# A fourth pair of output tiles by seven quarter products, with two pairs summed in PSUM

## The chip, the cores and the metric

The kernel runs on one core of a Trainium2 chip. TensorE multiplies, VectorE and ScalarE work on elements, GpSimd (POOL) and SyncE (SP) mostly start transfers. The metric is the device time of one execution in microseconds (us); the time of a kernel is the median of its runs.

## The reference

One decoder layer over 1024 tokens of width 1024, in float32:

```
h = rmsnorm(x) * (1 + scale(c)) + shift(c)
cv, cg, cs, lx, ls = split(h @ w_in)              # five blocks of 1024 columns
v = conv31(cv * sigmoid(cg))                      # causal, depthwise
v = silu(layernorm(v));  y_conv = (v @ pw2 + b) * silu(cs)
xs = conv4(lx);  r, i = sigmoid(xs @ wr), sigmoid(xs @ wi)     # eight heads
hs = scan(exp(-8 r softplus(-lam)), ...);  y_lru = hs * silu(ls)
x = x + (1 + gate(c)) * (concat(y_conv, y_lru) @ w_out)
out = rmsnorm(x, final_g)
```

The change is in the lru half of the last product, `y_lru @ w_out[1024:]`: eight output tiles of 128 channels by 1024 tokens, each a sum over eight blocks k of 128 rows of `w_out`.

## The kernel before

Channels lie on the partitions, tokens on the free axis; a half is 512 tokens, and one PSUM bank holds one half of a tile. Every float32 operand is split into a high part (`whi`, `yh`) and a remainder (`wlo`, `yl`), and a product is three matmuls: high by high (H), high by remainder (X), remainder by high (W). The order of all instructions on all engines comes from a planner written into the kernel (`Plan`): every operation has a priority (its slot number, with offsets), a cost, and the buffers that it reads and writes; the planner lays the operations out in time and emits them in that order. A PSUM tile `mm` has two banks (three such tiles), a tile `acc` has one (two of them); SBUF tiles come from a pool of 47 `big` buffers of 128x1024 and from smaller pools for weights (`raw`, `whi`, `wlo`, two of each). The planner keeps a reader and a writer of one PSUM tile apart in time (`o.psum`, `clear`); the semaphores that the instructions really wait for are put in afterwards by the tile framework, which looks at tiles.

The stages in order of slots: input products and gates (slots 0 to 39), the lru half of the output product (slots 40 to 47), the product with `pw2` (48 to 55), the conv half of the output product (56 and on), the last normalisation. The layer norm over the convolved channels (`conv_sum`, `layer_norm`, tiles `mean`, `lnss`, `lnbc`) and the operands for `pw2` (`quarters`) are made on VectorE and ScalarE during slots 40 to 47.

Output tiles 0 to 5 are made in pairs (`lru_pair`, `LRU_P = 3`). In a pair, blocks k = 0 to 3 (`JS = (0, 1)`) go by a scheme of seven quarter products in place of eight: with rows in two groups, columns in two halves, and the weight combinations S1 to S4 (`lsh`, `lsl`, made early by `lru_prepare` and kept in HBM) and operand combinations T1 to T4 (`yhs`, `yls`, made by `lru_sums`), the products are 1 = A11 B11, z = A12 B21, y = S1 T1, 2 = S2 T2, 3 = S3 T3, s = S4 B22, 4 = A22 T4. Each is two blocks by three matmuls of 512 columns. Product x goes on accumulating 1, 2, 3, 4 in one bank, and after each step `use` adds the running sum into one of the four quarters of the SBUF tiles `acc`, on ScalarE (the first time, `LACT`) or VectorE. Blocks k = 4 to 7 (`rest`) are multiplied directly (letters p, q, r). The order of a pair is `LORDER = "p1zy2q3s4r"`. It uses three PSUM tiles: `lp` (both halves of the first output tile), `lx` (of its two banks only the first) and `ly` (an `acc` tile). Tiles 6 and 7 (slots 46, 47) are made directly, as `ps`: 8 blocks by 3 matmuls by 2 halves, 48 matmuls each. A finished `acc` tile is added to `accd` in HBM by a transfer from POOL (`acc_store`).

A remainder is made either by VectorE (`SUB`) or by ScalarE and a transfer that adds (`remainder`): ScalarE writes minus the high part, POOL starts a transfer that adds the full value from HBM.

Of the kernel before, what the change touches and what calls it, by code (L numbers as in the profile page):

```python
# [14 lines left out]
P = 128  # L15
D = 1024
T = 1024
# [59 lines left out]
NP = {0: (6, 0, 1), 512: (6, 0, 7), 768: (6, 0)}  # L77
SUMS = (2, 0, 4, 3, 1, 6, 7, 5)
CSD = 2
SPILL = (0,2,4)  # L80
# [12 lines left out]
PREN, PRES = 5, 3  # L93
PREP, XCP = 18, 19
# [1 line left out]
XCN = 33  # L96
LEV = ()
LWB = "big"
LWO = 0.5
FINP = -0.5  # L100
BCLATE = False
BEHIND = 0
PLACED = ("big",)
MARGINS = 2.0
TERMS = {**{("pw2_0", c): ("HW", "X") for c in "1z"}, **{(f"out_{p}", "1"): ("HX", "W") for p in (0, 1, 2, 3)}, **{(f"pw2_{p}", "1"): ("HX", "W") for p in (1, 2, 3)}}
LTERMS = {}
LLATE = 45
SLOTT = {46: ("HX", "W"), 47: ("HX", "W")}
FINQ = 0.0
LRV = ()  # L110
QRES = 0
SINGLE = (0,)
AHEAD = 4
# [45 lines left out]
class Plan:  # L159
# [23 lines left out]
    def op(self, eng, cost, emit, prio, r=(), w=(), table=None, after=(), reserve=0,  # L183
           columns=0, lock=False, lag=0.0, moved=0.0, flight=FLIGHT):
        o = Op()
        o.lag, o.moved, o.flight = lag, moved, flight
        o.eng, o.cost, o.emit, o.prio, o.table = eng, cost, emit, prio, table
        o.succ, o.ready, o.seq, o.reserve = [], 0.0, len(self.ops), reserve
        o.columns = columns
        o.lock = not lag and eng == "POOL" or eng == "DVE" and lock  # L190
        r, w = list(self.keys(r)), list(self.keys(w))
        preds = set(after)
        for k in r:
            if k in self.writer:
# [166 lines left out]
def hymba_layer(ctx: ExitStack, tc: tile.TileContext, xT, vecs, mod_w, w_first, w_in,  # L361
# [214 lines left out]
    def mm_tile(name, parts=2):  # L576
        return S.buf("mm", name, F32, parts)
# [192 lines left out]
    def rstd(prio, sqs, a, e, ps, o, after=(), warm=(), idle=None):  # L770


        nb = (e - a) // P
        sd, rs = S.buf("sd", f"sd{prio}_{o}"), S.buf("rs", f"rs{prio}_{o}")
        wk = halves(ps, o, o + e - a)


        def warm_mm():
            pe.matmul(half(idle, 0)()[:, :P], ones, ones, start=True, stop=True)

        def stats(sq, k):
            for b in range(nb):
                pe.matmul(ps()[:, o + b:o + b + 1], sq()[:, a + b * P:a + b * P + P],
                          ones[:, 0:1], start=k == 0 and b == 0, stop=k == len(sqs) - 1,
                          skip_group_check=True)

        def spread(ps=ps):
            for b in range(nb):
                pe.matmul(ps()[:, o + b * P:o + b * P + P],
                          rs()[:, b:b + 1].to_broadcast([P, P]), ident, start=True, stop=True)  # L790
# [7 lines left out]
        inverse[a] = S.op("DVE", 0.2, lambda: dve.reciprocal(rs()[:, :nb], sd()[:, :nb]), prio, [sd], [rs])  # L798
# [478 lines left out]
    def gates(i, n):  # L1277
# [27 lines left out]
        o = split(B0 - 2 + 0.2 * i, yh[i], yl[i], t, reserve=SPARE)  # L1305
        if i < YHEADS:
            waiting.append(o)
        if LRU_P and i // 2 in JS:
# [2 lines left out]
                lru_sums(i // 2)  # L1311

    def lru_sums(j):
        pr, x0, x1 = B0 - 2 + 0.4 * j + LTP, ys[2 * j], ys[2 * j + 1]

        def sub(to, a, b):
            TT(pr, "DVE", half(*to), half(*a), half(*b), ALU.subtract, H, r=[a, b], w=[to])
        sub((x0, 0), (x0, 1), (x0, 0))
        sub((x0, 1), (x1, 1), (x0, 1))
        sub((x1, 1), (x1, 1), (x0, 0))  # L1320
        sub((x1, 0), (x1, 0), (x1, 1))
        sets = []
        for z, x in enumerate((x0, x1)):
            hi, lo = (big_buf(f"y{h}s{j}{z}", F32R, 2) for h in "hl")
            if j in LTD:
# [57 lines left out]
    def lru_pair(p, n, use, firsts):  # L1383
        rest = LK[2 * NJ:]
        s0, s1 = ("lru", 2 * p), ("lru", 2 * p + 1)
        q = n - 1.4 - LWO
        for s in (s0, s1):
            w_bufs(s, LWB)
            DMA(n - 2.5 - LWO, k3(raw[s]), lambda s=s: wsrc(s)[:, :, :], FULL_BYTES, w=[raw[s]])
        r0, r1 = raw[s0], raw[s1]  # L1390
        for s, k in ((s0, 0), (s1, NJ)):
            hi, lo, r = whi[s], wlo[s], raw[s]
            cut = lambda b, k=k: (lambda: k3(b)()[:, k:, :])
            keys = lambda b, k=k: [(b, i) for i in range(k, KT)]
            ACT(q, cut(hi), cut(r), "copy", (KT - k) * P, r=keys(r), w=keys(hi))
# [8 lines left out]
        for h, t in zip("hl", (sh, sl)):  # L1404
# [1 line left out]
        wq = {"S3": (sh, sl, 0, 0), "S4": (sh, sl, 1, 0), "S2": (sh, sl, 2, 0), "S1": (sh, sl, 3, 0),  # L1406
              "A11": (whi[s0], wlo[s0], 0, None), "A12": (whi[s0], wlo[s0], 1, None),
              "A22": (whi[s1], wlo[s1], 1, None)}
        p0, x, y = mm_tile(f"lp{p}"), mm_tile(f"lx{p}"), acc_tile(f"ly{p}")
        g, ops = 0.0, {}  # L1410

        def quarter(c, a, b, ps, h, begin):
            wh, wl, i, key = wq[a]
            rk = [(wh, key), (wl, key)] if key is not None else kk(wh, i) + kk(wl, i)
            for j, (bh, bl) in enumerate(lsets[b]):
                def emit(j=j, bh=bh, bl=bl):
                    o = (i * NJ + j) * P
                    for lhs, rhs, t in ((wh, bh, 0), (wh, bl, 1), (wl, bh, 2)):
                        pe.matmul(half(ps, h)(), lhs()[:, o:o + P], half(*rhs)(),  # L1419
                                  start=begin and j == 0 and t == 0, stop=j == NJ - 1 and t == 2,  # L1420
                                  skip_group_check=True)
                o = S.op("PE", 3 * (H + 32) / 2400, emit, n + g, [*rk, bh, bl],
                         [(ps, h if ps.parts > 1 else 0)], columns=3 * H)
                ops.setdefault(c, o)

        for c in LORDER:
            g += 0.12
            if c == "p":
                groups = LTERMS.get(p, ("HXW",))
# [90 lines left out]
    for s in slots[4:]:  # L1520
# [5 lines left out]
        if s[0] == "pair":  # L1526
# [14 lines left out]
            started[n], started[n + 1] = lru_pair(s[1], n, use, [started[n - 2]])  # L1541
            for m, t in zip((2 * s[1], 2 * s[1] + 1), ts):
                acc_store(n, m, t)
            n += 1
            continue
        if s not in NEXT:
            if s[0] == "lru":
                weights(s, n=n - LWO, eng="DVE" if s[1] in LRV else "DMA", where=LWB,
                        later=[started[LLATE]] if LLATE else [])
            else:  # L1550
                weights(s, late=[pending_evac[n]] if n in pending_evac else ())
# [243 lines left out]
```

## Time and profile before

| | |
|---|---|
| median of 3 runs | 726.79 us (726.64 to 727.24) |
| profiled execution | 726.9 us, of which the span of its instructions is 725.1 us |
| mean granted TensorE clock | 0.995 |
| TensorE matmuls | busy 717.0 us, 99% of the span |
| VectorE | 617.8 us, 85% |
| ScalarE | 480.8 us, 66% |
| lru half of the output product | from 470 to 558 us of the span |
| product with `pw2` | from 558 to 631 us |
| after the last conv products of 512 columns | from 704 us on |

Busy time of matmuls overlaps from one to the next: a matmul of 512 columns shows 389 ns, and the next one starts about 227 ns after it. How evenly TensorE is fed is read from the starts.

### The profile page before, as it was taken

To read this page: it belongs to the slowest core of one execution; us is meant where nothing else is said; L and a number is where in the kernel's file an instruction comes from. 1 tells how busy PE (TensorE), PEld (TensorE's weight loads), DVE (VectorE), ACT (ScalarE), POOL (GpSimd) and SP (SyncE) were. 2 spreads that over 40 slices of the span, in tenths; PEclk is the share of its full clock that TensorE was granted. 3 is DMA by queue.
4 is the path that set the end of the run, shared out by engine and by line. 5 is a ranking of instruction groups with operands and counts; after the bars stand their busy time and mean duration, and the time that the engine had idled before them with its cause. 6 is when DMAs were issued, how large, how long until landed. Compare 5 with 4: busy or idle time off the path is not lost.

```text
span 725.1 us, 9076 instructions
## 1 busy us (share of the span) xinstructions
PE 717.0 (99%) x3274; PEld 597.5 (82%) x3274; DVE 617.8 (85%) x848; ACT 480.8 (66%) x615; POOL 170.8 (24%) x172
## 2 busy tenths in 40 slices
PE   9999999999999999999999999999999999999996
PEld 8888888888888888888888888888888888888885
DVE  7999999899799997688499995999789566999656
ACT  7650679655698857966949879858785345755322
POOL 0036233443543320233220220211021101100003
PEclk9999999999999999999999999999999999999997
DMA  9946348768899997799999597998867855774006
GB/s 341 408 169 169 43 112 234 191 120 200 180 246 209 264 220 194 172 221 217 193 217 301 111 188 172 253 239 230 190 103 160 228 120 143 223 190 176 23 17 215
DMA packets 46059, 137.80 MB, mean 190 GB/s; under 512 B 5200, under 2 KB 15824, under 8 KB 45904
## 3 DMA queue, kind: packets, MB, share of 16 engines
q0 software_dynamic: 20016, 54.84, 42.0%
q1 hardware_dynamic: 24992, 81.48, 32.3%
q10 hardware_dynamic: 1008, 0.92, 0.4%
q8 instruction: 25, 0.41, 0.2%
q14 instruction: 18, 0.15, 0.1%
HBM read 79.37 MB, written 21.50 MB: 139 GB/s over the span
## 4 chain that ended last, share of the span: by engine, by line
PE 96%; DVE 1%; ACT 1%; DMA 1%; issue 0%; POOL 0%; POOLq 0%
PE ps L560 57%; PE xout L736 6%; PE xpw L736 6%; PE first L867 5%; PE ypw L736 3%; PE gate L1287 3%; PE lp L560 2%; PE lx L1419 2%; PE zout L736 2%; PE zpw L736 2%; PE ly L560 1%; PE lx L560 1%; PE lp L1419 1%; PE yout L736 1%; PE late L867 1%; PE ly L1419 1%
## 5 line engine op out<-in xcount | busy, mean ns | idle before, releaser
L560 PE MATMUL ps<-uh,whi 128*128 128x512 f32 x576 | 177.4, 389 | 0.0
L560 PE MATMUL ps<-ul,whi 128*128 128x512 f32 x576 | 177.4, 389 | 0.0
L560 PE MATMUL ps<-uh,wlo 128*128 128x512 f32 x576 | 177.3, 389 | 0.0
L560 PEld LDWEIGHTS ps<-uh,wlo 128*128 128x128 f32 x576 | 108.1, 188 | 22.5
L560 PEld LDWEIGHTS ps<-ul,whi 128*128 128x128 f32 x576 | 108.1, 188 | 22.4
L560 PEld LDWEIGHTS ps<-uh,whi 128*128 128x128 f32 x576 | 108.0, 188 | 22.3
L405 ACT CAST whi<-raw 128x1024 fp32r<-128x1024 f32 (+1 forms) x44 | 45.1, 1031 | 48.7 <-PE ps L560 30.0
L437 POOL DMA_DIRECT2D es<-cq x45 | 41.0, 910 | 128.7 <-ACT cq L413 90.2
L432 POOL TENSOR_TENSOR wlo<-raw,whi 128x1024 fp32r<-128x1024 f32 x16 | 41.6, 2607 | 88.6 <-ACT whi L405 88.3
L413 ACT ACT_TABLE_LOAD x45 | 57.7, 1283 | 2.0 <-PEq L1787 0.7
L424 DVE SCALAR_TENSOR_TENSOR cacc<-v,V,cacc 128x511 f32<-128x511 f32 (+14 forms) x75 | 55.8, 744 | 0.5
L424 DVE SCALAR_TENSOR_TENSOR caccs<-v,V,caccs 128x511 f32<-128x511 f32 (+6 forms) x70 | 52.1, 745 | 2.2 <-ACT caccs L413 1.1
L424 DVE SCALAR_TENSOR_TENSOR caccs<-c,wsum,caccs 128x511 f32<-128x511 f32 (+6 forms) x70 | 52.1, 745 | 0.8
L437 POOL DMA_DIRECT2D oo<-co x39 | 37.0, 980 | 41.3 <-issue 10.6
L413 ACT ACTIVATE cq<-v,V 128x511 f32<-128x511 f32 (+14 forms) x45 | 31.8, 709 | 0.0
L424 DVE SCALAR_TENSOR_TENSOR xs<-ps,V,xs 128x1023 f32<-128x1023 f32 (+2 forms) x24 | 30.7, 1278 | 0.0
L424 DVE SCALAR_TENSOR_TENSOR modw<-modw,sc 128x1024 f32<-128x1024 f32 x23 | 29.6, 1289 | 0.2 <-DMA modw<-in_mod_w_dram 0.2
L413 ACT ACTIVATE cq<-c,wsum 128x512 f32<-128x512 f32 x42 | 29.7, 713 | 0.0
L432 DVE TENSOR_TENSOR wlo<-raw,whi 128x1024 fp32r<-128x1024 f32 x20 | 24.4, 1220 | 5.4 <-ACT whi L405 5.2
L413 ACT ACTIVATE co<-v,V 128x510 f32<-128x510 f32 (+12 forms) x39 | 27.0, 707 | 0.0
L413 ACT ACTIVATE finsq<-fin 128x512 f32<-128x512 f32 (+2 forms) x14 | 7.9, 570 | 27.4 <-DVE fin L424 14.3
L432 POOL TENSOR_TENSOR o<-fin,bc 128x256 f32<-128x256 f32 (+1 forms) x8 | 7.8, 994 | 68.6 <-ACT bc L405 63.0
(413 smaller groups left out, 1585.5 us busy)
## 6 DMA issues: line engine op xcount, KB each, us to landing
raw<-in_w_in_dram SPq DMA_DIRECT2D x36, 512.0 KB, 5.5
modw<-in_mod_w_dram SPq DMA_DIRECT2D x24, 512.0 KB, 9.2
scsd<-scs SPq DMA_DIRECT2D x8, 512.0 KB, 3.7
raw<-in_w_out_dram SPq DMA_DIRECT2D x8, 512.0 KB, 7.7
accd<-acc POOLq DMA_DIRECT2D x8, 512.0 KB, 6.9
rawpw<-in_pw_dram SPq DMA_DIRECT2D x8, 512.0 KB, 4.3
scsr<-scsd SPq DMA_DIRECT2D x8, 512.0 KB, 4.5
rawout<-in_w_out_dram SPq DMA_DIRECT2D x8, 512.0 KB, 3.5
```

The lines of the kernel that those rows point to most:

```text
L405: act.copy(out(), in_())
L413: act.activation(out=out(), in_=in_(), func=func, **kw)
L424: dve.scalar_tensor_tensor(out=out(), in0=in0(), scalar=scalar, in1=in1(), op0=op0, op1=op1, accum_out=accum)
L432: lambda: e.tensor_tensor(out=out(), in0=a(), in1=b(), op=op), prio, r, w,
L437: return S.op("POOL", ISSUE, lambda: pool.dma_start(out(), a(), accum_op=ALU.add), prio, r, w, lag=RATE * n / T, after=after, flight=flight)
L560: pe.matmul(ps()[:, a - off:b - off], k3(lhs)()[:, at, :], rhs[k]()[:, a:b], start=(k == first and lhs is wh and rhs is xh and (a - off) % ...
L736: pe.matmul(half(ps, 0)(), half(*lhs)()[:, j * P:j * P + P], half(*rhs)(), start=start and at == 0 and i == 0, stop=at == len(order) - 1 a ...
L867: pe.matmul(ps()[:, a - off:b - off], fw_part(lhs, k, i * P, i * P + P)(), rhs()[:, a:b], start=k == 0 and lhs is wh and rhs is xh, stop=k ...
L1287: pe.matmul(ps()[:, c0:c1], lhs()[:, j, :], rhs()[:, c0:c1], start=st == 0, stop=st == 2)
L1419: pe.matmul(half(ps, h)(), lhs()[:, o:o + P], half(*rhs)(), start=begin and j == 0 and t == 0, stop=j == NJ - 1 and t == 2, skip_group_che ...
```

## The change

Four things are done. (1) Tiles 6 and 7 become a fourth pair (`LRU_P = 4`). (2) Pairs 2 and 3 (`FORKP`) no longer use `ly` and no longer add quarters up in SBUF: quarter product 1 is made in bank 0 of `lx` and copied by ScalarE into bank 0 of `lp`; y is made in bank 1 of `lx` and copied into an SBUF tile `lk`; 2 goes on in bank 0 of `lx`; VectorE adds `lx` bank 0 and `lk` into bank 1 of `lp`, and, after 3, into bank 1 of `lx`; z, s, 4 and the direct products then accumulate on these copies, and each finished output tile of 128x1024 is read out by one ScalarE instruction. For these two tiles the planner counts each bank for itself (`Bank`). (3) Some remainders move to VectorE: those of weights 3, 4, 5 (`LRV`) and of the lru operand combinations of j = 1 (`LTDMA` empty, `LTD` unused). (4) Numbers of the order: `TLATE` from 2.5 to 3.0, `LTP`, `LTJ`, `LWO`; weights of tiles 0 to 4 from the small pools (`LWBS`); groups of H and X before W in pairs 1 to 3 (`LTERMS`) and in some quarters of pair 0 (`QT`); the first four of the eight small matmuls that spread a norm over a tile now set the start flag once for each bank, so that a copy can be accumulated on afterwards.

```diff
-TLATE = 2.5
+TLATE = 3.0
-LRU_P = 3
+LRU_P = 4
-LTP = 0.5
+LORDERS = {}
+LTP = 0.0
+LTJ = (0.0, 0.4)
+LTDMA = ()
-LWO = 0.5
+LWO = 0.7
+FORKP = (2, 3)
+FORKN = -1.0
+FEVAC = ("ACT", "ACT")
+LWBS = (5, 6, 7)
-LRV = ()
+LRV = (3, 4, 5)
...
+        self.banks = None
+class Bank:
+    def __init__(self):
+        self.read, self.written = {}, {}
-        o.psum = [(b, any(k[0] is b for k in w)) for b in o.bufs if b.pool in ("mm", "acc")]
+        o.psum = [(b, any(k[0] is b for k in w)) for b in o.bufs if b.pool in ("mm", "acc") and not b.banks]
+        o.psum += [(k[0].banks[k[1]], k in w) for k in dict.fromkeys(r + w) if isinstance(k[0], Buf) and k[0].banks]
...
-        p0, x, y = mm_tile(f"lp{p}"), mm_tile(f"lx{p}"), acc_tile(f"ly{p}")
+        p0, x = mm_tile(f"lp{p}"), mm_tile(f"lx{p}")
+        y = None if p in FORKP else acc_tile(f"ly{p}")
...
+        if p in FORKP:
+            x.banks, p0.banks = [Bank(), Bank()], [Bank(), Bank()]
+            def both(h, to):
+                TT(n + FORKN, "DVE", half(to, 1), half(x, 0), half(kept, 0), ALU.add, H, r=[(x, 0), kept],
+                   w=[(to, 1)])
...
+            quarter("1", "A11", "B11", x, 0, True)
+            ACT(n + FORKN, half(p0, 0), half(x, 0), "copy", H, r=[(x, 0)], w=[(p0, 0)])
+            quarter("y", "S1", "T1", x, 1, True)
+            kept = big_buf(f"lk{p}")
+            ACT(n + FORKN, half(kept, 0), half(x, 1), "copy", H, r=[(x, 1)], w=[kept])
+            quarter("2", "S2", "T2", x, 0, False)
+            both(0, p0)
+            quarter("z", "A12", "B21", p0, 0, False)
+            plain(s0, p0, 0)
+            quarter("3", "S3", "T3", x, 0, False)
+            both(0, x)
+            quarter("s", "S4", "B22", p0, 1, False)
+            plain(s0, p0, 1)
+            out_of(0, p0)
+            quarter("4", "A22", "T4", x, 0, False)
+            plain(s1, x, 0)
+            plain(s1, x, 1)
+            out_of(1, x)
+            return ops["1"], ops["3"]
```

On TensorE nothing moves ahead of the first lru product, and from the second pair of `pw2` on the rows are the same. Pair 2 before, on TensorE, from its quarter product 1 (`lx`, the operands `yh_3782` and `yh_2187`) to its quarter product s (`lp` with the weights `lsh`); the bracket names the engine whose semaphore a row waits for:

```order
L1419 MATMUL lx_4235<-yh_3782,whi_4104 128x512 [waits Activation_49]
L1419 MATMUL lx_4235<-yh_2187,whi_4104 128x512
L1419 MATMUL lp_4199<-yh_3785,whi_4104 128x512
L1419 MATMUL ly_4145<-yhs_3806,lsh_4082 128x512
L1419 MATMUL lx_4235<-yhs_3866,lsh_4082 128x512 [waits Activation_49]
L1419 MATMUL lx_4235<-yhs_3819,lsh_4082 128x512
L1419 MATMUL lp_4199<-yh_3785,lsh_4082 128x512 [waits DVE_49]
```

(These are the first rows of seven groups of three; the rows between are the X and W matmuls of the same block.) Between the last row of product 1 and the row that waits for ScalarE stand nine matmuls of other tiles, and each of the two waits is for a tile that TensorE left some rows earlier. Pair 2 now, on TensorE, from the end of the first block of y (`lx` with `yhs_3814` and `lsh`, `lsl`) through its second block (`yhs_3047`) to the first block of 2 (`yhs_3849`):

```order
L1448 MATMUL lx_4179<-yhs_3814,lsl_4104 128x512 [waits DMAHW2_49]
L1448 MATMUL lx_4179<-yhs_3047,lsh_4100 128x512 [waits Activation_49]
L1448 MATMUL lx_4179<-yls_3062,lsh_4100 128x512
L1448 MATMUL lx_4179<-yhs_3047,lsl_4104 128x512
L1448 MATMUL lx_4179<-yhs_3849,lsh_4100 128x512
L1448 MATMUL lx_4179<-yls_3861,lsh_4100 128x512
L1448 MATMUL lx_4179<-yhs_3849,lsl_4104 128x512
L1448 MATMUL lx_4179<-yhs_3882,lsh_4100 128x512 [waits Activation_49]
```

and then, from the end of 2 (`yhs_3882`) through the first block of z (`lp` with `yh_3789`) to its second (`yh_3794`):

```order
L1448 MATMUL lx_4179<-yhs_3882,lsl_4104 128x512
L1448 MATMUL lp_4193<-yh_3789,whi_4088 128x512
L1448 MATMUL lp_4193<-yl_3806,whi_4088 128x512
L1448 MATMUL lp_4193<-yh_3789,wlo_4098 128x512
L1448 MATMUL lp_4193<-yh_3794,whi_4088 128x512 [waits DVE_49]
```

Product 1 of `lx` is now followed by y in the other bank of the same tile; the waits stand in the middle of y, of 2 and of z, between two blocks of one product, and no matmul of another tile is between. What is waited for, on ScalarE, in the same place (`lp_4193<-lx_4179` copies product 1, `lk_4205<-lx_4179` copies y):

```order
L433 ACTIVATE acc_4133<-lx_4059,gate_95 128x512 [waits PE_49]
L425 COPY lp_4193<-lx_4179 128x512 [waits PE_49,Activation_49]
L433 ACTIVATE wlo_4200<-whi_4175 128x768 [waits DMAHW6_49]
L425 COPY lk_4205<-lx_4179 128x512 [waits PE_49]
L433 ACTIVATE lnsq_4211<-c_3093 128x1024 [waits DVE_49]
```

Both copies are new, and each waits for TensorE. In the built program the first one waits for the count that is raised by the matmul `lx_4179<-yhs_3814,lsl_4104` (the third of y, in bank 1), not by the last matmul of product 1 in bank 0, which stands three matmuls earlier; the second one waits for the third matmul of 2 (`yhs_3849,lsl_4104`), not for the end of y. The addition on VectorE that fills bank 1 of `lp` (`lp_4193<-lx_4179,lk_4205`) waits for the third matmul of z. In pair 3 the copy into `lp` stands in the same way; the copy into `lk` waits for the end of 2 and holds up no matmul at once; the addition into `lp` waits for the end of z, and the next matmul waits for the addition.

More of the change, by code (lines that the diff above doesn't have):

```diff
@@ L79 @@
 CSD = 2
-SPILL = (0,2,4)
+SPILL = (0, 2, 4)
 SPP0, SPP1, SPN = 30, 40.5, 39
@@ L102 @@
 BEHIND = 0
+FORKP = (2, 3)
+FORKN = -1.0
+FEVAC = ("ACT", "ACT")
+FEVN = 0.3
+QT = {(0, c): ("HW", "X") for c in "y234"}
 PLACED = ("big",)
 MARGINS = 2.0
+LSN = 1
+LWBS = (5, 6, 7)
+LWG = 0
 TERMS = {**{("pw2_0", c): ("HW", "X") for c in "1z"}, **{(f"out_{p}", "1"): ("HX", "W") for p in (0, 1, 2, 3)}, **{(f"pw2_{p}", "1"): ("HX", "W") for p in (1, 2, 3)}}
-LTERMS = {}
+LTERMS = {p: ("HX", "W") for p in (1, 2, 3)}
 LLATE = 45
@@ L1381, in acc_store, with lru_pair @@
         ADD(n + 0.5, lambda: acc_d[m], t, r=[t, ("accd", m)], w=[("accd", m)], flight=LAND)
-    def lru_pair(p, n, use, firsts):
+    def lru_pair(p, n, use, firsts, tiles):
         rest = LK[2 * NJ:]
@@ L1394, in lru_pair @@
             keys = lambda b, k=k: [(b, i) for i in range(k, KT)]
-            ACT(q, cut(hi), cut(r), "copy", (KT - k) * P, r=keys(r), w=keys(hi))
+            ACT(q, cut(hi), cut(r), "copy", (KT - k) * P, r=keys(r), w=keys(hi),
+                after=[started[n - LWG]] if LWG and p else [])
             if s[1] in LRV:
@@ L1414, in quarter, with emit @@
             rk = [(wh, key), (wl, key)] if key is not None else kk(wh, i) + kk(wl, i)
-            for j, (bh, bl) in enumerate(lsets[b]):
-                def emit(j=j, bh=bh, bl=bl):
+            groups = QT.get((p, c), ("HXW",))
+            order = [(g_, j) for g_ in groups for j in range(NJ)]
+            for at, (g_, j) in enumerate(order):
+                bh, bl = lsets[b][j]
+                terms = [{"H": (wh, bh), "X": (wh, bl), "W": (wl, bh)}[t] for t in g_]
+                def emit(j=j, at=at, terms=terms):
@@ L1417, in emit @@
                     o = (i * NJ + j) * P
-                    for lhs, rhs, t in ((wh, bh, 0), (wh, bl, 1), (wl, bh, 2)):
+                    for t, (lhs, rhs) in enumerate(terms):
                         pe.matmul(half(ps, h)(), lhs()[:, o:o + P], half(*rhs)(),
-                                  start=begin and j == 0 and t == 0, stop=j == NJ - 1 and t == 2,
+                                  start=begin and at == 0 and t == 0,
+                                  stop=at == len(order) - 1 and t == len(terms) - 1,
@@ L1421, in emit @@
                                   skip_group_check=True)
-                o = S.op("PE", 3 * (H + 32) / 2400, emit, n + g, [*rk, bh, bl],
-                         [(ps, h if ps.parts > 1 else 0)], columns=3 * H)
+                rd = [x for x in rk if x[0] is wh and g_ != "W" or x[0] is wl and "W" in g_]
+                rd += [bh] * (g_ != "X") + [bl] * ("X" in g_)
+                o = S.op("PE", len(g_) * (H + 32) / 2400, emit, n + g, rd,
+                         [(ps, h if ps.parts > 1 else 0)], columns=len(g_) * H)
@@ L1424, in quarter, with plain, out_of @@
                 ops.setdefault(c, o)
-        for c in LORDER:
+        if p in FORKP:
+            x.banks, p0.banks = [Bank(), Bank()], [Bank(), Bank()]
+            def plain(s, ps, h):
+                for k in rest:
+                    mm_k(n + g, ps, s, yh, yl, k, FULL[h:h + 1], first=-1)
+            def both(h, to):
+                TT(n + FORKN, "DVE", half(to, 1), half(x, 0), half(kept, 0), ALU.add, H, r=[(x, 0), kept],
+                   w=[(to, 1)])
+            def out_of(i, ps):
+                m = 2 * p + i
+                if FEVAC[i] == "ACT":
+                    ACT(n + FEVN + i, tiles[i], ps, AF.Copy, scale=gate1[:, m:m + 1], r=[ps, ("gate1", m)],
+                        w=[tiles[i]])
+                else:
+                    TS(n + FEVN + i, tiles[i], ps, gate1[:, m:m + 1], None, ALU.mult, r=[ps, ("gate1", m)],
+                       w=[tiles[i]], n=T)
+            quarter("1", "A11", "B11", x, 0, True)
+            ACT(n + FORKN, half(p0, 0), half(x, 0), "copy", H, r=[(x, 0)], w=[(p0, 0)])
+            g = 0.1
+            quarter("y", "S1", "T1", x, 1, True)
+            kept = big_buf(f"lk{p}")
+            ACT(n + FORKN, half(kept, 0), half(x, 1), "copy", H, r=[(x, 1)], w=[kept])
+            g = 0.2
+            quarter("2", "S2", "T2", x, 0, False)
+            both(0, p0)
+            g = 0.3
+            quarter("z", "A12", "B21", p0, 0, False)
+            plain(s0, p0, 0)
+            g = 0.4
+            quarter("3", "S3", "T3", x, 0, False)
+            both(0, x)
+            g = 0.5
+            quarter("s", "S4", "B22", p0, 1, False)
+            plain(s0, p0, 1)
+            out_of(0, p0)
+            g = 0.6
+            quarter("4", "A22", "T4", x, 0, False)
+            plain(s1, x, 0)
+            g = 0.7
+            plain(s1, x, 1)
+            out_of(1, x)
+            return ops["1"], ops["3"]
@@ L1427, in lru_pair @@
+        for c in LORDERS.get(p, LORDER):
             g += 0.12
@@ L1547, in hymba_layer @@
             if s[0] == "lru":
-                weights(s, n=n - LWO, eng="DVE" if s[1] in LRV else "DMA", where=LWB,
+                weights(s, n=n - LWO, eng="DVE" if s[1] in LRV else "DMA",
+                        where=LWB if s[1] in LWBS else None,
                         later=[started[LLATE]] if LLATE else [])
```

16 lines of the change are left out of this document (10 added, 6 removed).

## The prediction

> **What bounds the kernel now.** I read the page first, for the engine that fills the span, then the list of waits and the chain of waits, to see whether that engine ever stands.
>
> ```profile
> span 725.1 us, 9076 instructions
> PE 717.0 (99%) x3274; PEld 597.5 (82%) x3274; DVE 617.8 (85%) x848; ACT 480.8 (66%) x615; POOL 170.8 (24%) x172
> PEclk9999999999999999999999999999999999999997
> PE 96%; DVE 1%; ACT 1%; DMA 1%; issue 0%; POOL 0%; POOLq 0%
> ```
>
> TensorE matmuls cover 99% of the span at nearly full clock, and 96% of the chain that ends last lies on TensorE. The list of waits of TensorE has two entries, one at each end of the program:
>
> ```profile
> PE token_stats L824 <- DVE ones L482: 1.1, 1, 1.1
> PE finbc L789 <- DVE rs65.7_0_5820 L798: 0.9, 1, 0.9
> ```
>
> So between the first and last microseconds TensorE is fed all the time. Its rate is read from a group of the chain:
>
> ```profile
> 339.52 2.72 PE gate L1287 x12
> ```
>
> Twelve matmuls of 512 columns in 2.72 us: one starts every 0.2267 us. In this kernel a matmul removed is worth 0.2267 us, and a gap between two starts is lost from the end time, one for one. Since a busy row shows 0.39 us, a short gap is hidden in busy time, so I read the starts through the lru half. There is one gap, in the timeline of TensorE, with the ScalarE row of the same moment behind it (start, duration, engine, line, operation):
>
> ```profile
> 476.50 0.39 PE L1419 MATMUL ly<-yhs,lsl 128*128 128x512 f32 x1
> ...
> 477.18 0.39 PE L1419 MATMUL lx<-yhs,lsl 128*128 128x512 f32 x1
> 477.66 0.50 PE L560 MATMUL ly<-yh,whi 128*128 128x512 f32 x1
> 478.00 0.39 PE L560 MATMUL ly<-yl,whi 128*128 128x512 f32 x1
> 478.23 0.39 PE L560 MATMUL ly<-yh,wlo 128*128 128x512 f32 x1
> 476.92 0.69 ACT L413 ACTIVATE acc<-ly,gate 128x512 f32<-128x512 f32 x1 [1.77 <-PE ly L1419]
> ```
>
> This is the measuring stick for the whole prediction. The last matmul into `ly` ends at 476.50 + 0.39 = 476.89; ScalarE starts 0.03 us later, reads for 0.69 us until 477.61; the next matmul into `ly` starts 0.05 us after that, at 477.66. The three matmuls of `lx` between cover most of this; the next start would have been 477.41, so 0.25 us are lost, and the matmul behind starts after 0.34 us in place of 0.23, another 0.11. Together 0.36 us.
>
> **The change: matmuls.** Tiles 6 and 7 were made directly:
>
> ```profile
> L560 PE MATMUL ps<-yl,whi 128*128 128x512 f32 x32 | 9.9, 389 | 0.0
> L560 PE MATMUL ps<-yh,whi 128*128 128x512 f32 x32 | 9.8, 389 | 0.0
> L560 PE MATMUL ps<-yh,wlo 128*128 128x512 f32 x32 | 7.6, 389 | 0.0
> ```
>
> These are 96 matmuls. A pair takes seven products of two blocks by three matmuls, 42, and directly for k = 4 to 7 two tiles by two halves by four blocks by three, 48: together 90. Six go: 6 x 0.2267 = 1.36 us. The gap at `ly` depends on three covering matmuls and one ScalarE row; in the new order nothing of pairs 2 and 3 uses `ly`, and ScalarE has moved, so I take it as gone: 0.36 us. The gain is 1.72 us.
>
> **The change: waits.** The bookkeeping by bank is the planner's; the order of the built program shows that the semaphores are still by tile. Five waits of TensorE have no other tile's work to do meanwhile. In pair 2: in the middle of y for the copy `lp<-lx`, in the middle of 2 for the copy `lk<-lx`, in the middle of z for the addition `lp<-lx,lk`. In pair 3: in the middle of y for the copy `lp<-lx`, and ahead of the direct products for the addition into `lp`. Each has the same form: the other engine cannot start before TensorE's last matmul ends, and TensorE does nothing until the other engine ends. What stands behind the waiting matmul on TensorE is everything, since its queue runs in order. The trace of before has neither of the two operations in this place; the nearest rows by engine, source and size are these (count, total, mean ns):
>
> ```profile
> L405 ACT COPY rbc<-token_stats 128x512 f32<-128x512 f32 x2 | 1.2, 586 | 1.4 <-PE token_stats L1002 1.4
> L413 ACT ACTIVATE acc<-ly,gate 128x512 f32<-128x512 f32 x6 | 4.1, 680 | 6.3 <-PE lx L1419 2.6 <-PE ly L560 1.9 <-PE ly L1419 1.8
> L432 DVE TENSOR_TENSOR yc<-ypw,yc 128x512 f32<-128x512 f32 x4 | 2.8, 688 | 0.1
> L424 DVE SCALAR_TENSOR_TENSOR acc<-lx,gate,acc 128x512 f32<-128x512 f32 x6 | 4.5, 746 | 0.2 <-PE lx L1419 0.2
> ```
>
> The copy from PSUM of 512 columns takes 0.59 us by the same operation, 0.68 at most by the ScalarE row with a scale; the addition of PSUM and SBUF 0.69 us, 0.75 at most by the row with a scale. I take 0.59 and 0.69, the same operations. A copy wait then costs, by the measuring stick: 0.39 (the matmul's end) + 0.03 + 0.59 + 0.05 - 0.23 (the start that was due anyway) + 0.11 (the slow start behind) = 0.94 us. An addition wait: 0.94 + 0.10 = 1.04 us. Three copies and two additions: 2.82 + 2.08 = 4.90 us. Bounds: without the slow start 4.90 - 5 x 0.11 = 4.35; with 0.68 and 0.75 it is 4.90 + 3 x 0.09 + 2 x 0.06 = 5.29.
>
> Against this stands a rule that would make the waits cost nothing. The Trainium skill, "Perfetto Trace Analysis", section "Matmuls", says that independent matmul groups should rotate through PSUM banks so that reading one out overlaps the next one's matmuls. The new code does go to the other bank; by the rule the sum would be the gain alone. The gap at 477.41 does not decide this, since there `ly` is a tile of its own and one bank; the order does, and it has TensorE wait for the other bank's reader.
>
> **The change: the rest, at nothing.** Ahead of the first lru product and from the second pair of `pw2` on TensorE's rows stay. Remainders moved to VectorE, the earlier `lru_prepare` of the fourth pair with its transfers on the queues of POOL and SP, and the reads of 128x1024 on ScalarE (18 or more matmuls, 4 us, before that bank pair is written again) lie beside TensorE's work. They matter only where VectorE must deliver to TensorE, and that is the layer norm. Its spread `lnbc` stands some ten us later in TensorE's order, and the operands of `pw2` hang on it:
>
> ```profile
> 513.73:558.40 44.67, 42.39 (x53) 1.00 0.66 129
> 513.77 1.22 DVE L432 TENSOR_TENSOR cr<-cr,lnbc 128x1024 f32<-128x1024 f32 x1 [2.76 <-PE lnbc L789]
> 514.91 1.21 DVE L432 TENSOR_TENSOR c<-c,lnbc 128x1024 f32<-128x1024 f32 x1
> 516.04 1.21 DVE L432 TENSOR_TENSOR cr<-cr,lnbc 128x1024 f32<-128x1024 f32 x1
> ...
> 522.83 0.69 DVE L432 TENSOR_TENSOR vu<-cr 128x512 f32<-128x512 f32 x1
> 523.43 0.69 DVE L432 TENSOR_TENSOR vt<-c,cr 128x512 f32<-128x512 f32 x1
> ...
> 558.40 1.22 DVE L432 TENSOR_TENSOR vlb<-c,vhb 128x1024 fp32r<-128x1024 f32 x1
> ```
>
> The first row is VectorE's busy time from the spread to the last early operand: 2.28 us idle in 44.67. Spacing is 1.13 us for 128x1024 (514.91 to 516.04) and 0.60 for 128x512 (522.83 to 523.43). In the new order there stand on VectorE, from the spread to the `vlb` that `pw2` waits for, 17 of the large and 32 of the small: 19.2 + 19.2 = 38.4, with the same idle time 40.7 us. TensorE has 179 matmuls there, 40.6 us, and the two waits of pair 3, 2.0: 42.6. VectorE arrives some 2 us early: no cost, with little to spare.
>
> **Sum.** -1.72 + 4.90 = +3.18 us. The profiled execution of before took 726.9 us, 725.1 of it the span; the new one would take 730.1. The median of before is 726.79, 0.1 below its profiled execution, so I give the median as **730.0 us**.
>
> **Rivals.**
> *The waits cost next to nothing.* If the copies overlap the matmuls of the other bank, or each waits on an older count than I read, only the gain is left: 726.8 - 1.7 = 725.1. For it: the banks are different. Against: the waits as built. Chance 0.06. This is the outcome by the rule of the Trainium skill named above ("Perfetto Trace Analysis", section "Matmuls").
> *Half of it.* The other engine starts earlier, or TensorE resumes at once: 0.2 to 0.45 us a wait, 1.0 to 2.2 in all; 726.1 to 727.3, within 0.2% (1.45 us, about what a measurement of this kernel can tell from no change). Against: 0.59 and 0.69 are execution times, and nothing lies beside them. Chance 0.06.
> *The layer norm comes late.* My slack of 2 us rests on VectorE's idle time staying at 2.3 us. VectorE now also waits for TensorE in pair 3 and carries more remainders; if it loses 4 us more, `pw2` starts 2 us late: 732.0, up to 732.4. It decides from 2 us of added work on. Chance 0.12.
> *The clock falls.* Five drains within 30 us might make the throttle lower the clock. The rows with TensorE idle part of the time speak against (us, busy of PE, PEld, DVE, ACT, POOL, clock, DMA share, GB/s), and one row for it is the first matmuls' spread of durations:
>
> ```profile
> 0.00:3.40 3.40, 2.34 (x10) 2.20 (x11) 0.77 (x5) 2.00 (x4) 0.70 (x6) 1.00 0.45 117
> 476.00:479.40 3.40, 3.30 (x15) 2.38 (x15) 3.30 (x5) 2.48 (x3) 0.00 (x0) 1.00 0.90 313
> 713.60:717.00 3.40, 2.86 (x24) 2.59 (x23) 2.83 (x9) 1.35 (x4) 1.77 (x3) 1.00 0.33 117
> L824 PE MATMUL token_stats<-ones x24: 275/275/582, 1.1 to 7.2; 128*128 128x128 f32 x24
> ```
>
> At 713.6 TensorE lacks 0.54 of 3.40 us, and the granted clock is 1.00; the gap at 477 left it at 1.00 too. But the same small matmul takes 275 ns, or 582 at the start. At half the speed a stretch of 3.4 us (15 matmuls x 0.227) takes 3.4 us more: 730.0 + 3.4 = 733.4. Chance 0.05. The Trainium skill, "TensorE: Matmul & The Clock Gate", section "A second HAM failure mode: psum-queue depth-cycling", reports just that: small idle times between groups that cycle through PSUM banks make the clock go up and down. In the windows above the trace does not agree.
>
> **How the numbers follow.** The forecast, five full waits, has 0.71; with the four rivals that makes 1. The forecast's own range goes from 726.79 - 1.72 + 4.35 = 729.4 to 726.79 - 1.36 + 5.29 = 730.7 (the gap at `ly` staying in another place). Below it I allow for one wait partly covered (-0.6): **728.8**. Above it I take in the late layer norm, up to **732.4**. Outside are the two rivals below and the clock, 0.17. Faster by over 0.2%: 0.06. Within: 0.06. Slower: the rest, 0.88.
>
> **What would show it.** In the new trace there should be 3268 matmuls; after the third matmul of y, in pairs 2 and 3, a gap of about 1.17 us between two starts in place of 0.23, with a ScalarE copy `lp<-lx` of about 0.59 us inside it; the same for `lk<-lx` in the middle of 2 in pair 2, and 1.27 us around each VectorE addition `lp<-lx,lk`. TensorE's list of waits should gain these entries, about 0.6 to 1 us each, and the end should come rigidly later by their sum less 1.7 us. I am wrong if the starts go on every 0.23 us through these places (the semaphores are then finer than the order shows), if a new wait stands at the first products of `pw2`, or if the granted clock in the 3.4 us windows after the waits is below 1.00.

## The result, and the profile after

| | before | changed |
|---|---|---|
| median (first set) | 727.22 us (726.64 to 727.58, 6 runs) | 732.45 us (731.90 to 733.59, 6 runs) |
| ratio | | 1.0075, 95% interval 1.0062 to 1.0088 |
| same kernels, a second set (E9) | 727.15 us (15 runs) | 732.02 us (731.60 to 732.82, 5 runs), ratio 1.0069, 1.0055 to 1.0082 |
| profiled execution, its span | 726.9 us, 725.1 us | 731.9 us, 730.1 us |

The change makes the kernel slower by 5 us. Forecast were 3.2 us more, 730.0, with a range up to 732.4: the direction holds, the size is short by some 2 us. (The 732.45 lie 2.45 above the 730.0; 0.43 of it is that the kernel before has 727.22 in these runs and had 726.79 in those that the forecast counts from.) The page of the changed kernel, the same lines as before the change:

```profile
span 730.1 us, 9057 instructions
PE 717.0 (98%) x3268; PEld 595.6 (82%) x3268; DVE 619.3 (85%) x851; ACT 481.0 (66%) x618; POOL 170.3 (23%) x172
PEclk9999999999999999999999999999999999999998
PE 85%; DVE 6%; ACT 4%; issue 3%; DMA 1%; DVEq 0%; POOLq 0%; ACTq 0%
```

Six matmuls are gone, and TensorE's busy time is the same 717.0 us: busy time does not show the gaps. TensorE's share of the chain that ends last falls from 96 to 85%. Its list of waits names where (what waits, for what, total, times, longest); the two entries at the ends of the program are as before and left out:

```profile
PE ly L580 <- DMA wlo<-in_w_out_dram: 1.5, 1, 1.5
PE lx L1448 <- ACT lp L425: 1.4, 2, 0.7
...
PE lp L1448 <- DVE lp L452: 0.9, 1, 0.9
PE lp L580 <- DVE lp L452: 0.9, 1, 0.9
PE lx L1448 <- ACT lk L425: 0.7, 1, 0.7
```

Five waits are the predicted ones: three for copies, two for additions. The first, 1.5 us for a transfer, was in no part of the prediction.

The timeline of TensorE through pair 2, with the three rows of ScalarE and VectorE for which it stands, shows the form of the five waits:

```profile
515.40 0.39 PE L1448 MATMUL lx<-yhs,lsl 128*128 128x512 f32 x1
516.50 0.50 PE L1448 MATMUL lx<-yhs,lsh 128*128 128x512 f32 x1 [0.71 <-ACT lp L425]
516.84 0.40 PE L1448 MATMUL lx<-yls,lsh 128*128 128x512 f32 x1
...
517.76 0.39 PE L1448 MATMUL lx<-yhs,lsl 128*128 128x512 f32 x1
518.83 0.50 PE L1448 MATMUL lx<-yhs,lsh 128*128 128x512 f32 x1 [0.68 <-ACT lk L425]
...
520.09 0.40 PE L1448 MATMUL lp<-yh,wlo 128*128 128x512 f32 x1
521.35 0.50 PE L1448 MATMUL lp<-yh,whi 128*128 128x512 f32 x1 [0.86 <-DVE lp L452]
515.88 0.57 ACT L425 COPY lp<-lx 128x512 f32<-128x512 f32 x1 [0.92 <-PE lx L1448]
518.19 0.59 ACT L425 COPY lk<-lx 128x512 f32<-128x512 f32 x1 [0.98 <-PE lx L1448]
520.60 0.70 DVE L452 TENSOR_TENSOR lp<-lx,lk 128x512 f32<-128x512 f32 x1 [3.95 <-PE lp L1448]
```

The copy of product 1 (bank 0) starts only behind the third matmul of y (bank 1), which ends at 515.79; TensorE goes on 0.05 us after the copy's end. From start to start it is 1.10, 1.07 and 1.26 us in place of 0.23, and the start behind is late by another 0.11 each time (516.50 to 516.84 in place of 0.23). Pair 3 has one copy and one addition of the same lengths:

```profile
542.60 0.39 PE L1448 MATMUL lx<-yhs,lsl 128*128 128x512 f32 x1
543.64 0.50 PE L1448 MATMUL lx<-yhs,lsh 128*128 128x512 f32 x1 [0.66 <-ACT lp L425]
...
546.96 0.39 PE L1448 MATMUL lp<-yh,wlo 128*128 128x512 f32 x1
548.21 0.50 PE L580 MATMUL lp<-yh,whi 128*128 128x512 f32 x1 [0.86 <-DVE lp L452]
```

The excess of the five is 0.87 + 0.84 + 1.03 + 0.81 + 1.02 = 4.57, with five slow starts 5.1 us; 4.90 were forecast. The sixth gap lies in pair 0, where TensorE comes to the remainder of weight 1 (the columns of ScalarE's and POOL's rows are the same; the last row is the group of that transfer, 384 KB, with the time from its issue to its landing):

```profile
481.14 0.39 PE L580 MATMUL ly<-yl,whi 128*128 128x512 f32 x1
483.03 0.50 PE L580 MATMUL ly<-yh,wlo 128*128 128x512 f32 x1 [1.50 <-DMA wlo<-in_w_out_dram]
469.96 0.84 ACT L425 CAST whi<-raw 128x768 fp32r<-128x768 f32 x1
471.61 0.84 ACT L433 ACTIVATE wlo<-whi 128x768 fp32r<-128x768 f32 x1
473.11 0.87 POOL L457 DMA_DIRECT2D wlo<-in_w_out_dram  x1 [9.75 <-PE lx L1448]
wlo<-in_w_out_dram POOLq DMA_DIRECT2D x1, 384.0 KB, 9.9
```

It costs 1.89 - 0.23 + 0.11 = 1.77 us. The transfer lands at 473.11 + 9.9 = 483.0, and the matmul that needs it was due at 481.37. Before the change the same two steps were ten to eleven us earlier, from the same views of the kernel before:

```profile
460.16 0.83 ACT L405 CAST whi<-raw 128x768 fp32r<-128x768 f32 x1
462.27 0.87 POOL L437 DMA_DIRECT2D wlo<-in_w_out_dram  x1 [4.15 <-ACT wlo L413]
```

The reason stands in the change: `LWBS = (5, 6, 7)` puts both parts of weight 1 into the small pools `whi` and `wlo`, of two buffers each, where they were in the large pool. In the built program ScalarE's cast therefore waits for the last matmul that still reads the old content, in the last input product. In the trace that matmul ends at 469.7, and the cast begins at 469.96 with no idle time of ScalarE in front of it: the planner has put it into ScalarE's queue behind the moment when the buffer comes free. One small late arrival is left in the product with `pw2`, 0.27 us, where `zpw` waits for VectorE's `vlb`:

```profile
571.01 0.39 PE L756 MATMUL ypw<-vha,l34pw 128*128 128x512 f32 x1
571.40 0.50 PE L756 MATMUL zpw<-vlb,whipw 128*128 128x512 f32 x1
571.74 0.39 PE L756 MATMUL ypw<-vha,h34pw 128*128 128x512 f32 x1
```

**Sum.** 5.1 + 1.77 + 0.27 - 1.36 - 0.36 = +5.4 us. The first matmul of the final norm moves by 5.8 us, 0.4 more than the sum (first and last start, in the rows of the tile `finbc`, before and changed):

```profile
L783 PE MATMUL finbc<-ones,finss x16: 168/250/250, 700.7 to 714.8; 128*128 128x1 f32 x16
L803 PE MATMUL finbc<-ones,finss x16: 168/250/250, 706.5 to 720.6; 128*128 128x1 f32 x16
```

Of the 0.4 us, 0.1 lies ahead of the output products (the first input product starts at 54.9 us before and at 55.0 after); the rest shows no gap of its own and stays open. (In the kernel before, the last conv product ends at 698.5 us; the 704 in the table ahead is too late.) The end moves by 5.0 us only, since the last stretch is 0.8 us shorter (725.1 - 700.7 = 24.4, 730.1 - 706.5 = 23.6), which has to do with the clock (last section).

### The profile page after: what moved, and what is told of

It is laid out like the page before. It is cut to its first block, busy times and chain, and to the rows that moved or that the text cites. A ratio compares the mean times of both kernels' runs of the same rounds, so it can differ in the third digit from the quotient of the medians.

```text
span 730.1 us, 9057 instructions
## 1 busy us (share of the span) xinstructions
PE 717.0 (98%) x3268; PEld 595.6 (82%) x3268; DVE 619.3 (85%) x851; ACT 481.0 (66%) x618; POOL 170.3 (23%) x172
## 4 chain that ended last, share of the span: by engine, by line
PE 85%; DVE 6%; ACT 4%; issue 3%; DMA 1%; DVEq 0%; POOLq 0%; ACTq 0%
PE ps L580 43%; PE xout L756 6%; PE xpw L756 6%; PE first L889 5%; PE lx L1448 3%; PE ypw L756 3%; PE lp L580 2%; PE lx L580 2%; PE gate L1309 2%; DVE caccs L444 2%; PE y L726 2%; PE zpw L756 2%; PE zout L756 1%; DMA wlo<-in_w_out_dram 1%; PE lp L1448 1%
## 5 line engine op out<-in xcount | busy, mean ns | idle before, releaser
L452 DVE TENSOR_TENSOR wlo<-raw,whi 128x1024 fp32r<-128x1024 f32 (+1 forms) x23 | 27.4, 1194 | 8.4 <-ACT whi L425 8.4
L444 DVE SCALAR_TENSOR_TENSOR modw<-modw,sc 128x1024 f32<-128x1024 f32 x23 | 31.4, 1369 | 0.2 <-DMA modw<-in_mod_w_dram 0.2
```

The lines of the kernel that those rows point to most:

```text
L444: dve.scalar_tensor_tensor(out=out(), in0=in0(), scalar=scalar, in1=in1(), op0=op0, op1=op1, accum_out=accum)
L452: lambda: e.tensor_tensor(out=out(), in0=a(), in1=b(), op=op), prio, r, w,
```

## The experiments

Theory A: the five waits come from semaphores by tile and cost what the timeline shows, and the transfer of weight 1's remainder is late because of the small buffer. Rival B: the pairs lose time because ScalarE or VectorE is behind, and the waits would move elsewhere. Rival C: the transfer is late because the queues are full, whatever the buffer. The kernels of one group share their runs of the kernel before: 727.37 us for E1 to E4, 727.12 for E5 to E8, 727.15 for E9 and E10.

**E1, no copies in PSUM.**

```diff
-FORKP = (2, 3)
+FORKP = ()
```

> All four pairs go by the old scheme (FORKP empty), everything else as changed. Theory A (the five waits of pairs 2 and 3 cost 5.1 us, and the late remainder of weight 1 costs 1.8): the five gaps go, the wait for the transfer stays, so 732.5 - 5.1 = 727.4, within 0.2% of before, and up to 0.4 more where a wait at ly returns. Rival B (the pairs lose time to ScalarE and VectorE being behind, not to the waits by tile): the gaps move to other places and it stays at 731 or above.

Measured: 734.26 us (733.80 to 734.67), ratio 1.0095 (1.0081 to 1.0110). The five gaps are gone, the wait for the transfer is still there, and the time is 2 us longer, not 5 shorter. By itself E1 fits rival B (gaps in other places, 731 or above) as well as theory A; E3 decides between them. TensorE's list of waits has three new entries, in the product with `pw2`:

```profile
PE ypw L756 <- ACT vha L425: 1.8, 1, 1.8
PE ly L580 <- DMA wlo<-in_w_out_dram: 1.6, 1, 1.6
PE ypw L756 <- DVE vla L452: 1.4, 1, 1.4
...
PE zpw L756 <- DVE vlb L452: 0.8, 1, 0.8
```

This is the late layer norm of the prediction's rivals. VectorE's groups from the spread `lnbc` to the last `vla` that `pw2` waits for (523.4 to 573.3 here, 528.7 to 572.0 in the changed kernel) show why; first three of E1, then two of the changed kernel (count, busy, mean ns, idle before and for what):

```profile
L444 DVE SCALAR_TENSOR_TENSOR acc<-lx,gate,acc 128x512 f32<-128x512 f32 x4 | 3.0, 745 | 0.0
L444 DVE SCALAR_TENSOR_TENSOR acc<-lp,gate,acc 128x512 f32<-128x512 f32 x4 | 3.0, 745 | 0.0
L452 DVE TENSOR_TENSOR vla<-cr,vha 128x512 fp32r<-128x512 f32 x3 | 2.1, 693 | 4.9 <-PE lx L1448 4.8
```

```profile
L452 DVE TENSOR_TENSOR lx<-lx,lk 128x512 f32<-128x512 f32 x2 | 1.4, 693 | 0.0
L452 DVE TENSOR_TENSOR lp<-lx,lk 128x512 f32<-128x512 f32 x1 | 0.7, 700 | 1.7 <-PE lp L1448 1.7
```

The old scheme puts eight additions, 6.0 us, among the layer norm's work, the new one three, 2.1 us, and VectorE stood 4.8 us for a product of the pair. The same two views have one more difference: of the weights of `pw2` (`rawpw`, `l34pw`) VectorE made 9.1 us of work in E1's stretch, 5.8 in that of the changed kernel. `pw2` started to lose time at 569, over 6 us with the lower clock that followed (0.78 and 0.72 in the two windows behind the gap). So E1 does not tell the price of the waits. It shows that without the copies in PSUM VectorE is late for `pw2`; how much of this is the additions, the standing and the weights is not separated.

**E2, weight 1 in the large pool.**

```diff
-LWBS = (5, 6, 7)
+LWBS = (1, 5, 6, 7)
```

> As changed, but the parts of weight 1 get buffers of the large pool, as before the change (LWBS = 1, 5, 6, 7). Theory A (the remainder of weight 1 comes late because its high part has to wait for a small buffer until the last input product ends): its transfer is started some 10 us earlier, the wait of 1.5 us goes, 732.5 - 1.8 = 730.7. Rival C (the transfer is late because the queues are full at that time, whatever the buffer): still a wait for the transfer, 732 or more.

Measured: 731.07 us (730.20 to 732.86), ratio 1.0053 (1.0041 to 1.0065), 1.4 us less than the changed kernel; the two intervals just touch, so the size of the gain is uncertain. The transfer starts at 465.53, and no matmul waits for it: against rival C.

```profile
465.53 0.87 POOL L457 DMA_DIRECT2D wlo<-in_w_out_dram  x1 [1.28 <-ACT wlo L433]
```

The profiled execution is the longest of the five (span 731.1) and shows no gain: a new wait of 1.2 us for VectorE's addition into `acc` came up in pair 1 (the order of TensorE differs from the changed kernel's from pair 0 on), the clock was at 0.56 in the window from 522.2 to 525.6, behind the copies of pair 2, and the first input product already starts 0.9 us later (55.9 in place of 55.0).

**E3, one-bank tiles.** Each bank of `lx` and `lp` of pairs 2 and 3 is a tile of its own, and the finished tiles are read out in halves.

```diff
+            X = [(acc_tile(f"lx{p}_{i}"), 0) for i in (0, 1)]
+            L = [(mm_tile(f"lp{p}_{i}"), 0) for i in (0, 1)]
...
-            ACT(n + FORKN, half(p0, 0), half(x, 0), "copy", H, r=[(x, 0)], w=[(p0, 0)])
+            ACT(n + FORKN, half(*L[0]), half(*X[0]), "copy", H, r=[X[0]], w=[L[0]])
```

> As changed, but in pairs 2 and 3 each bank of lx and lp is a tile of its own (two acc tiles and half of two mm tiles), and finished tiles are read out in two halves. Order and number of matmuls stay. Theory A (the waits are by tile): the five gaps of about 1.2 us go, 732.5 - 5.1 = 727.4. Rival B: the gaps stay, since the copy or the addition itself is needed at once; 731 to 732.5.

Measured: 728.54 us (727.59 to 731.14), ratio 1.0024 (1.0014 to 1.0034): 3.9 us less than the changed kernel. TensorE's list of waits:

```profile
PE ly L581 <- DMA wlo<-in_w_out_dram: 1.8, 1, 1.8
...
PE lx L1449 <- ACT acc L434: 0.8, 1, 0.8
```

All five are gone, with the same copies and additions made: against rival B. TensorE's order is the changed kernel's too: in the two traces the 3268 matmuls agree, by the names of their tiles, in all but 20 places, and these lie in `pw2`. The forecast was 727.4. One new wait of 0.8 us in the list (ScalarE still reads a one-bank tile of pair 2 into `acc` when pair 3 wants it) costs 1.1 us from start to start with the slow restart, which is the difference.

**E4, both cures**: E3 with `LWBS = (1, 5, 6, 7)`.

> One-bank tiles in pairs 2 and 3 and weight 1 in the large pool. Theory A: both losses go, 732.5 - 5.1 - 1.8 = 725.6, which is the six matmuls and the gap at ly below the kernel before (727.2 - 1.7 = 725.5): faster by 0.2%. Rival (the two gaps cover each other, or another operand is late next): 726.5 to 728.

Measured: 725.77 us (724.84 to 726.13, 10 runs), ratio 0.9976 (0.9967 to 0.9985): faster than before the change, and 0.2 from the forecast. The list of waits is down to the two of the kernel before; a gap that the list does not have stands at the third matmul of pair 0 (rows of the timeline behind it):

```profile
PE token_stats L847 <- DVE ones L503: 1.1, 1, 1.1
PE finbc L810 <- DVE rs65.7_0_5842 L821: 0.9, 1, 0.9
470.05 0.39 PE L1449 MATMUL lx<-yl,whi 128*128 128x512 f32 x1
470.52 0.50 PE L1449 MATMUL lx<-yh,wlo 128*128 128x512 f32 x1
470.87 0.40 PE L1449 MATMUL lx<-yh,whi 128*128 128x512 f32 x1
```

It costs 0.36 us, as much as the gap at `ly` did. The matmul needs the remainder of weight 0, whose transfer starts at 462.26 and takes 8.2 us from issue to landing; in the changed kernel it takes 5.9. The transfer of weight 1 now starts 2.2 us behind it and runs beside it. In the six kernels of this study that are made so, weight 0's transfer takes 7.8 to 8.9 us; in the five where weight 1 comes later or without a transfer, 5.5 to 6.6. So the cure of the one transfer makes the other slower: rival C is wrong for weight 1, but what runs beside a transfer does count.

**E5, the copies wait again**: E4 with `lx` of two banks.

> As the kernel with both cures (one-bank tiles, weight 1 in the large pool), but lx of pairs 2 and 3 is one tile of two banks again. The waits for the two copies of pair 2 stand in the middle of y and of 2 again; in pair 3 some fifty matmuls of other tiles now lie between product 1 and y, so that wait has cover. Theory A (a wait by tile costs about 0.95 us where TensorE has nothing else): 725.8 + 2 x 0.95 = 727.7. If every copy cost its time, covered or not: 725.8 + 3 x 0.95 = 728.6. Rival B (waits are not it): 725.8.

Measured: 738.32 us (737.71 to 739.76), 10.6 more than forecast. The copies of pair 2 cost what was said (0.7 us in the list for each, 0.93 and 0.96 by the starts), and the covered one of pair 3 nothing. But the planner also laid out another order, with new waits: 1.5 us for ScalarE's and 1.2 for VectorE's work on `acc`, 0.8 for the remainder of weight 0. The largest is of 4.0 us: pair 3's product 1 moved ahead, and behind it pair 2's product 3 waits for the addition of pair 2, which stands on VectorE behind the layer norm. The timeline of TensorE, then of VectorE:

```profile
531.03 0.39 PE L1449 MATMUL lx<-yh,wlo 128*128 128x512 f32 x1
535.43 0.79 PE L1449 MATMUL lx<-yhs,lsh 128*128 128x512 f32 x1 [4.02 <-DVE lp L453]
531.17 3.47 DVE L453 TENSOR_TENSOR c<-c,lnbc 128x1024 f32<-128x1024 f32 x3
534.68 0.70 DVE L453 TENSOR_TENSOR lp<-lx,lk 128x512 f32<-128x512 f32 x1
535.40:538.80 3.40, 3.37 (x8) 2.69 (x9) 2.78 (x5) 3.40 (x6) 0.00 (x0) 0.50 0.00 0
```

A wait costs the other engine's queue too, not its operation alone: 4 us here, where the operation takes 0.70. This wait is for the bank itself, which the addition reads and product 3 goes on in, so a tile for each bank would not spare it, and the total of E5 is not a price of the copies. The last row is a window: the clock is at 0.50 behind this gap.

**E6, the additions wait again**: E4 with `lp` of two banks.

> As the kernel with both cures, but lp of pairs 2 and 3 is one tile of two banks again. TensorE then waits for VectorE's addition into the other bank, once in each pair. Theory A: 725.8 + 2 x 1.15 = 728.1, down to 727.2 if the eight small matmuls of the norm cover most of the one in pair 2. Rival B: 725.8.

Measured: 727.21 us (726.15 to 727.95), at the forecast's lower end. The list has one addition wait of 0.9 us, in pair 3 (1.13 by the starts; 1.15 were forecast for one); at the one of pair 2 there is no gap: the small matmuls of the norm stand there. TensorE's order is E4's but for 30 places in `pw2`.

**E7, three pairs**: E4 with `LRU_P = 3` and `FORKP = (2,)`.

> As the kernel with both cures, but with three pairs: tiles 6 and 7 are made directly again (six matmuls of 512 columns more). Theory A: 725.8 + 6 x 0.2267 = 727.1. Rival (the matmuls saved are not worth their full time, since something else comes late there): 725.8 to 726.5; or, if VectorE and the transfers have more time with three pairs, less.

Measured: 727.87 us (726.92 to 728.63), 2.1 more than E4. In the profiles, from the first `ps` to the first `xout` it is 1.6 us more: 1.36 for the six matmuls and 0.25 that TensorE stood longer for the remainder of weight 0. The rest is the last stretch, which was the long kind (24.3 us from `finbc` to the end, 23.6 in E4), and the start.

**E8, the remainder of weight 1 on VectorE.**

```diff
-LRV = (3, 4, 5)
+LRV = (1, 3, 4, 5)
```

> The changed kernel, but the remainder of weight 1 is made by VectorE from the loaded weight, without a transfer (LRV = 1, 3, 4, 5); its high part still waits for the small buffer. Theory A (what comes late is the transfer that adds, 9.9 us long, behind a high part that is late): the wait of 1.8 us goes, 732.5 - 1.8 = 730.7, with the five waits left. Rival C (the late high part alone makes it late): a wait of some 1.5 us at the same matmul, now for VectorE, 732.

Measured: 730.10 us (729.94 to 730.78). Nothing waits for the remainder, though its high part still waits for the small buffer: it is the late high part and the 9.9 us of the transfer together. There are four waits in pairs 2 and 3 here (the addition of pair 2 is covered) and one of 0.6 us for VectorE in pair 1.

**E9, the changed kernel again.**

> The changed kernel once more. Open is what makes its median 0.55 us longer than the profiled execution. Theory A: the five gaps are alike in every execution (5.1 us), and the length of the transfer of weight 1's remainder varies: its gap in a second profile differs from 1.8 us by as much as the times differ. Rival: the granted clock, which would show in the clock of the longer runs (0.003 less for some 2 us).

Measured: 732.02 us (731.60 to 732.82). The five gaps agree with the first profile to 0.01 us; the gap for the transfer is 2.04 us, not 1.77, and the span 730.3, not 730.1. The clock of its runs is 0.996 or 0.997, without order. So the transfer varies; that it makes the whole spread is not shown.

**E10, E4 with the remainder of weight 2 on VectorE** (`LRV = (2, 3, 4, 5)`).

> The kernel with both cures, and the remainder of weight 2 on VectorE too (LRV = 2, 3, 4, 5): the gap of 0.36 us that was left there, ahead of the first matmul that needs this remainder, goes: 725.8 - 0.4 = 725.4. Rival: VectorE is late elsewhere by the added 1.1 us (the operands of the product with pw2), 725.8 to 727.

Measured: 726.28 us (725.71 to 726.82), ratio 0.9989 (0.9980 to 0.9998): not better than E4. The gap stays (0.32 us): it stands ahead of the third matmul of pair 0, which needs the remainder of weight 0 (see E4), not of weight 2, so the expectation named the wrong weight. And the wait for ScalarE's reading of `acc` as in E3 is back (0.7 us).

## Why the prediction was right and wrong

- **Six matmuls, 1.36 us:** right; E7 puts them back and is 1.6 us longer from the first `ps` to the first `xout`, of which 0.25 is a longer gap. **The gap at `ly`, 0.36 us:** it went, but with the waits cured (E4) a gap of the same size stands in pair 0. E4's median is 1.6 us below the kernel before, close to the 1.72; this is partly luck. In the profiles E4 gains 1.2 us between these two points (54.9 to 631.2 before, 54.8 to 629.9 in E4), and 0.8 us come from the last stretch (24.4 and 23.6 us), which the prediction did not have.
- **Five waits by tile, 4.90 us:** right in place, cause and size, 5.1 measured. The operations took 0.57 to 0.59 and 0.70 us, as in the rows that were taken. That the tile and not the work is the cause is shown by E3: the same operations and the same order there on TensorE, other tiles, no gap.
- **The rule on rotating banks:** the code did go to the other bank and the gaps came all the same, so the outcome by the rule of the Trainium skill ("Perfetto Trace Analysis", section "Matmuls") did not come; with a tile for each bank (E3) it did.
- **"The change: the rest, at nothing":** this step failed. It said that transfers and buffers lie beside TensorE's work and matter only through VectorE and the layer norm. The weights that went to the small pools were listed in the change, but no row was read for when these buffers come free. Weight 1's high part moved from 460.16 to 469.96, behind the last reader of its buffer, and its remainder landed 1.6 us after the matmul that needs it was due. The missing term is +1.8 to 2.0 us (the changed kernel's two profiles), which brings 730.0 to 732; E2 and E8 each take the wait away, the one by the buffer, the other by the way in which the remainder is made.
- **The layer norm late:** 0.27 us came of it in the changed kernel. That there is little to spare was right: E1, with 3.9 us more of additions and 3.3 more of weights on VectorE in that stretch, lost over 6 us there. The rival had it from 2 us on. The range reached up to 732.4 for this rival; that the time came out beside that end has another cause.
- **The last stretch:** 0.8 us shorter in both profiles of the changed kernel than before, in no part of the prediction. It hides 0.8 us of the loss, so the miss of some 2 us is smaller than what TensorE lost beyond the sum (5.8 us at the final norm in place of 3.18).
- **The clock:** full (1.00) in both profiles of the changed kernel after the five gaps. In E1 and E5 it fell after longer gaps (2.2 and 1.9 us in a row; 4.4 us); in E2 it fell behind two gaps like those of the changed kernel, and why is open.

## What to carry to other kernels

Where two engines share a PSUM tile, look at which instruction the built program waits for, not at banks: bookkeeping by bank in a planner does not reach the semaphores, and a tile for each bank removed five waits of together 5.1 us here (3.9 us in the time, since another wait came up). Price a drain as the end of the matmul, the other engine's queue, its operation and a slow restart; about 1 us each for 512 columns, if the queue is empty. When a buffer moves from a large pool to a small one, find the last reader of what is in it, and follow the load, the cast and the transfer from there to the first use. Then look at what else is in flight: a transfer that starts earlier can make its neighbour late.

## What was not expected of the hardware

- The restart: the prediction took it from one gap; it turned out to be the same everywhere. Behind each gap the first matmul shows 0.50 us and the next start comes after 0.34 us, not 0.23. This 0.11 us came behind every wait between matmuls of 512 columns that was looked at here at full clock, whether of 0.2 or 1.9 us.
- The clock at half: after stretches with gaps, single windows of E1, E2 and E5 show a granted clock of 0.50 to 0.80 and starts 0.43 us apart (E5: 536.02, the next at 536.45). How much idle time does it is not shown: in the changed kernel TensorE is busy for 2.41 of 3.40 us in the window from 517.4, and the clock stays at 1.00; in E2 the two windows ahead of the fall have 2.74 and 2.73. In E3 the three runs above 730 us have a mean clock of 0.994, the others 0.995 to 0.998.
- The last stretch varies by 0.8 us. From the first `finbc` to the end the same work takes 24.4 us before and 23.6 in the changed kernel; E7 has 24.3, E1 24.1, E8 23.8, the others 23.5 or 23.6. The windows around the last matmuls (columns as above), before and changed:

```profile
717.80:721.20 3.40, 1.34 (x7) 1.05 (x5) 2.44 (x6) 0.37 (x1) 1.41 (x2) 0.50 0.92 302
723.60:727.00 3.40, 0.72 (x7) 0.53 (x5) 2.44 (x6) 0.37 (x1) 1.41 (x2) 0.74 1.03 340
```

Seven matmuls take 1.34 us at a clock of 0.50 and 0.72 us where part of the window has the full clock. So the length goes by whether the clock steps down ahead of these matmuls or behind them. What sets that moment is not shown. Up to 0.8 us of a comparison can come from there, though the work of this stretch is the same.
